# Split weight tiles laid out by parity, and the two matmuls of every second wide tile exchanged

## The chip, the cores and the metric

The kernel runs on one core of a Trainium2 chip. The time is that of the device in microseconds (us), the median of three executions; one further execution was taken with the hardware profiler. TensorE (PE in the profile) multiplies and has a second row, PEld, for its weight loads; VectorE (DVE) and ScalarE (ACT) work elementwise; SyncE (SP) issues the transfers. 

## The reference, cut to what matters

Two layers, each of a half-step SwiGLU feed-forward block, a mixer and a second feed-forward block, then a last norm. x has 256 positions of 1024 channels, float32.

```python
def swiglu_ffn(h, w_up, w_down):
    u = h @ w_up                      # 1024 -> 2 * 2816
    a, b = jnp.split(u, 2, axis=-1)
    return (jax.nn.silu(a) * b) @ w_down

for l in range(DEPTH):                # DEPTH = 2
    x = x + 0.5 * swiglu_ffn(rmsnorm(x, norm_ffn1[l]), ffn1_w_up[l], ffn1_w_down[l])
    x = x + hybrid_mixer(rmsnorm(x, norm_mix[l]), ...)   # in-projection, pooling, RG-LRU, gates, out-projection
    x = x + 0.5 * swiglu_ffn(rmsnorm(x, norm_ffn2[l]), ffn2_w_up[l], ffn2_w_down[l])
return rmsnorm(x, final_norm)
```

All matrices together are 3152 tiles of 128x128 float32 values, and each is used once.

## The kernel before, in words

Activations lie transposed: channels on the 128 partitions, the 256 positions along the free dimension. Every matrix tile is the stationary operand of TensorE (the weights), and the activations stream past it as the moving operand. Products are made in fp32r from two halves: each weight tile w is split into a high half wh (ScalarE, a copy that rounds to fp32r) and a low half wl = w - wh (VectorE), and each activation x into xh and xl in the same way. Three products count: wh*xh, wh*xl and wl*xh.

There are two forms of a tile's work. The wide form (`mm_wide`, feed-forward blocks and the mixer's last projection) uses that xh and xl of a block lie side by side: one matmul wl with the 256 columns of xh (L330), and one matmul wh with all 512 columns of xh and xl (L331), both into one PSUM bank; the sums of the bank's two halves are added later. The narrow form (`mm`, nearly all of the mixer) has three matmuls of 256 columns: wh*xh, wh*xl, wl*xh (L317, L318, L319). Each of these matmuls is preceded by a weight load of its own (LDWEIGHTS), which PE takes up while the matmul before it is still streaming.

The weights come in the order of their use, 8 tiles to a chunk (`CHUNK`), one DMA per chunk into one of 5 raw buffers (`NRAW`); a chunk is then split by one ScalarE and one VectorE instruction into one of 8 pairs of buffers wh and wl (`NSPL`). A matmul waits for its chunk's split, and a split waits until PE has gone through the chunk that had the buffer before.

The order of all instructions is made ahead by a planner (`Plan.schedule`) that simulates the engines with given durations: PE and the DMA queue keep the order of the program, ScalarE and VectorE take the ready operation with the longest work behind it.

Places in SBUF: the pool of the wh buffers comes first (each 4096 bytes a partition, a tile 512 bytes), then a filler of `SHIFT` = 112 floats (448 bytes), then the wl buffers, then XS, the activations of the block in work, and the other moving operands, each a multiple of 256 bytes long. Counted modulo 256 bytes, wl tiles lie where the moving operands lie, and wh tiles 64 bytes past it: from wh to wl there are 8 x 4096 + 448 bytes, which is 192 modulo 256, and from wl to XS 8 x 4096, which is 0.

The lines that the text names are L317 to L319 in `mm`, L330 and L331 in `mm_wide`, L220 (ScalarE) and L229 (VectorE) in the helpers, and L361, the norm's sum over channels, a float32 matmul that is put between two wide tiles.

Of the kernel before, what the change touches and what calls it, by code (L numbers as in the profile page):

```python
# [9 lines left out]
F32R = mybir.dt.float32r  # L10
# [25 lines left out]
CHUNK = 8  # L36
HEAD = [[2, 2, 4], [4, 4], [4, 4], [4, 4]]
NRAW = 5
NSPL = 8
SHIFT = 112  # L40
WARM = 7


# [155 lines left out]
class Trunk:  # L199
# [62 lines left out]
    def chunk(self, q):  # L262

        prev = self.raws[q - NRAW] if q >= NRAW else None
        raw = Buf(self.plan, lambda: self.env.rawp.tile([128, CHUNK * 128], F32, tag="raw", name="raw"), prev)
        prev_h, prev_l = self.spl[q - NSPL] if q >= NSPL else (None, None)
        hi = Buf(self.plan, lambda: self.env.whp.tile([128, CHUNK * 128], F32R, tag="wh", name="wh"), prev_h)
        lo = Buf(self.plan, lambda: self.env.wlp.tile([128, CHUNK * 128], F32R, tag="wl", name="wl"), prev_l)
        self.raws.append(raw)
        self.spl.append((hi, lo))  # L270
        return raw, hi, lo

    def chunk_run(self, q, o, n, d):
        raw = self.raws[q]
        hi, lo = self.spl[q]

        def load():
            self.env.nc.sync.dma_start(  # L278
                out=raw.t[:, o * 128:(o + n) * 128],
                in_=self.env.wts[d * 16384:(d + n) * 16384].rearrange("(p f) -> p f", p=128))  # L280

        s = slice(o * 128, (o + n) * 128)
        self.dma_in(load, 0.182 * n, [(raw, o)])
        self.split(lambda: hi.t[:, s], lambda: lo.t[:, s], lambda: raw.t[:, s], [(raw, o)], [(hi, o)], [(lo, o)], n * 128)
        for i in range(o, o + n):
            self.where.append((q, o, i))

# [12 lines left out]
    def next_tile(self, tag):  # L300
        c = len(self.order)
        self.order.append(tag)
        while c >= len(self.where):
            self.more_weights()
        q, o, i = self.where[c]
        hi, lo = self.spl[q]
        s = slice(i * 128, (i + 1) * 128)
        return lambda: hi.t[:, s], lambda: lo.t[:, s], [(hi, o), (lo, o)]

    def mm(self, tag, ps, half, xh, xl, r, start, stop):  # L310

        wh, wl, keys = self.next_tile(tag)

        def fn():
            t = self.env.nc.tensor
            out = ps.t[:, half, :]
            t.matmul(out, lhsT=wh(), rhs=xh(), start=start, stop=False)  # L317
            t.matmul(out, lhsT=wh(), rhs=xl(), start=False, stop=False)  # L318
            t.matmul(out, lhsT=wl(), rhs=xh(), start=False, stop=stop)  # L319

        self.plan.add("PE", T_MM, fn, keys + list(r), [(ps, half)])

    def mm_wide(self, tag, ps, x, r, start, stop):

        wh, wl, keys = self.next_tile(tag)

        def fn():
            t = self.env.nc.tensor

            t.matmul(ps.t[:, 0, :], lhsT=wl(), rhs=x()[:, 0, :], start=start, stop=False, skip_group_check=True)  # L330
            t.matmul(ps.t, lhsT=wh(), rhs=x(), start=False, stop=stop, skip_group_check=True)  # L331

        self.plan.add("PE", T_MM_WIDE, fn, keys + list(r), [(ps, 0), (ps, 1)])

# [44 lines left out]
    def x(self, m):  # L379
        return self.X.t[:, KD + m * S:KD + (m + 1) * S]  # L380
# [457 lines left out]
@with_exitstack  # L838
def tile_trunk(ctx: ExitStack, tc: tile.TileContext, xt: bass.AP, par: bass.AP, wts: bass.AP, out: bass.AP):
    trunk = Trunk()  # L840
    env = Env()
    env.nc, env.xt, env.par, env.wts, env.out = tc.nc, xt, par, wts, out
    env.one = ctx.enter_context(tc.tile_pool(name="one", bufs=1))
    env.rawp = ctx.enter_context(tc.tile_pool(name="rawp", bufs=NRAW))
    env.whp = ctx.enter_context(tc.tile_pool(name="whp", bufs=NSPL))


    ctx.enter_context(tc.tile_pool(name="shift", bufs=1)).tile([128, SHIFT], F32, name="shift")
    env.wlp = ctx.enter_context(tc.tile_pool(name="wlp", bufs=NSPL))
    env.xsp = ctx.enter_context(tc.tile_pool(name="xsp", bufs=1))  # L850
    env.big = ctx.enter_context(tc.tile_pool(name="big", bufs=1))
    env.psp = ctx.enter_context(tc.tile_pool(name="psp", bufs=8, space=bass.MemoryType.PSUM))
    trunk.env = env
    with tc.manual_schedule():
        for op in trunk.plan.schedule():
            op.fn()
# [52 lines left out]
```

## Time and profile before

| what | us |
|---|---|
| median of three executions | 1120.95 |
| the three | 1120.82, 1120.95, 1125.40 |
| the profiled execution | 1125.55 |
| its span, first to last instruction | 1123.8 |
| PE busy | 1111.3 |
| VectorE busy | 885.0 |
| ScalarE busy | 691.1 |

Wide tiles: 2218. Narrow tiles: 934. In a timeline, the start of a matmul tells more than its length: matmuls are pipelined, so the recorded lengths overlap, and the time that a matmul takes on PE is from its start to the start of the next one. A window count of a line includes the instruction that was already running when the window began.

### The profile page before, as it was taken

Reading aid. Unit: us, or ns where it says so; the run is one execution under the profiler, and the core shown is the slowest. Engines: PE = TensorE matmul, PEld = TensorE weight load, DVE = VectorE, ACT = ScalarE, POOL = GpSimd, SP = SyncE. Lnnn points to the kernel's source line nnn. Section 1 sums busy time; section 2 is a strip of 40 time slices with the busy share of each in tenths; the row PEclk is TensorE's granted clock in tenths of the full one; section 3 lists DMA queues with packets and bytes.
Section 4 is the critical chain, followed back from the end, with each engine's and each line's share of the span. In section 5 each row is a group of like instructions: output and inputs, shape, how many; then the busy total and the mean of one; then the engine's idle time right before and its main releaser. Section 6 shows DMA issues by size and latency. Waiting matters only on the chain.

```text
span 1123.8 us, 18938 instructions
## 1 busy us (share of the span) xinstructions
PE 1111.3 (99%) x7268; PEld 1017.0 (91%) x7268; DVE 885.0 (79%) x1384; ACT 691.1 (62%) x1133; POOL 0.2 (0%) x4
## 2 busy tenths in 40 slices
PE   8999999999999999999999999999999999999996
PEld 7888888999999888888888888899999998888886
DVE  7998766898987877776678887679989788777652
ACT  8766655568865755555566566555687666555541
POOL 0000000000000000000000000000000000000000
PEclk9999999999999999999999999999999999999999
DMA  8856666556556666666666666666475565656531
GB/s 286 264 171 206 189 188 188 184 174 200 188 183 192 182 192 188 187 188 188 187 188 195 197 190 192 198 188 190 141 227 183 183 197 184 189 187 189 188 107 38
DMA packets 59130, 210.03 MB, mean 187 GB/s; under 512 B 6560, under 2 KB 7456, under 8 KB 59040
## 3 DMA queue, kind: packets, MB, share of 16 engines
q1 hardware_dynamic: 59040, 208.82, 59.7%
q8 instruction: 57, 0.93, 0.3%
q14 instruction: 33, 0.27, 0.1%
HBM read 207.75 MB, written 1.05 MB: 186 GB/s over the span
## 4 chain that ended last, share of the span: by engine, by line
PE 98%; DVE 0%; DMA 0%; ACT 0%; SPq 0%; DVEq 0%; issue 0%; ACTq 0%
PE ps L331 45%; PE ps L330 23%; PE ps L318 10%; PE ps L317 10%; PE ps L319 10%; DMA XG<-in_x 0%; PE ps L361 0%; DVE XF L229 0%; DVE rt L371 0%; ACT XS L220 0%; SPq L278 0%; SPq L792 0%; PE ps L367 0%; DVE wl L229 0%; ACT wh L220 0%; DVEq L904 0%
## 5 line engine op out<-in xcount | busy, mean ns | idle before, releaser
L220 ACT ACTIVATE wh<-raw 128x1024 fp32r<-128x1024 f32 (+2 forms) x399 | 418.0, 1050 | 364.1 <-PE ps L331 271.3
L229 DVE TENSOR_TENSOR wl<-raw,wh 128x1024 fp32r<-128x1024 f32 (+2 forms) x399 | 481.8, 1210 | 184.9 <-ACT wh L220 183.4
L331 PE MATMUL ps<-XS,wh 128*128 128x512 f32 x1408 | 491.7, 394 | 0.0
L330 PE MATMUL ps<-XS,wl 128*128 128x256 f32 x1408 | 396.2, 281 | 2.5 <-DVE wl L229 2.5
L331 PEld LDWEIGHTS ps<-XS,wh 128*128 128x128 f32 x1408 | 265.5, 189 | 58.4
L330 PEld LDWEIGHTS ps<-XS,wl 128*128 128x128 f32 x1408 | 267.6, 190 | 3.7 <-DVE wl L229 3.6
L317 PE MATMUL ps<-XS,wh 128*128 128x256 f32 x640 | 180.2, 282 | 0.0
L318 PE MATMUL ps<-XS,wh 128*128 128x256 f32 x640 | 179.9, 281 | 0.0
L319 PE MATMUL ps<-XS,wl 128*128 128x256 f32 x640 | 179.9, 281 | 0.0
L317 PEld LDWEIGHTS ps<-XS,wh 128*128 128x128 f32 x640 | 122.8, 192 | 0.1
L318 PEld LDWEIGHTS ps<-XS,wh 128*128 128x128 f32 x640 | 120.2, 188 | 0.1
L319 PEld LDWEIGHTS ps<-XS,wl 128*128 128x128 f32 x640 | 120.1, 188 | 0.0
L331 PE MATMUL ps<-GA,wh 128*128 128x512 f32 x341 | 119.9, 393 | 0.0
L331 PE MATMUL ps<-GB,wh 128*128 128x512 f32 x341 | 119.9, 393 | 0.0
L330 PE MATMUL ps<-GB,wl 128*128 128x256 f32 x341 | 95.4, 280 | 0.0
L330 PE MATMUL ps<-GA,wl 128*128 128x256 f32 x341 | 95.4, 280 | 0.0
L331 PEld LDWEIGHTS ps<-GA,wh 128*128 128x128 f32 x341 | 64.0, 188 | 14.1
L331 PEld LDWEIGHTS ps<-GB,wh 128*128 128x128 f32 x341 | 64.1, 188 | 14.0
L229 DVE TENSOR_TENSOR FT<-ps,FT 128x256 f32<-128x256 f32 x176 | 72.8, 416 | 2.4 <-ACT FT L220 2.4
L220 ACT ACTIVATE FT<-ps 128x256 f32<-128x256 f32 x176 | 64.1, 366 | 6.1 <-PE ps L331 5.8
L330 PEld LDWEIGHTS ps<-GB,wl 128*128 128x128 f32 x341 | 64.6, 189 | 0.0
L330 PEld LDWEIGHTS ps<-GA,wl 128*128 128x128 f32 x341 | 64.5, 189 | 0.0
(127 smaller groups left out, 1228.7 us busy)
## 6 DMA issues: line engine op xcount, KB each, us to landing
raw<-in_w SPq DMA_DIRECT2D x390, 512.0 KB, 4.1
raw<-in_w SPq DMA_DIRECT2D x7, 256.0 KB, 5.4
XG<-in_x SPq DMA_DIRECT2D x3, 256.0 KB, 5.1
out<-XF SPq DMA_DIRECT2D x3, 256.0 KB, 2.2
raw<-in_w SPq DMA_DIRECT2D x2, 128.0 KB, 3.1
out<-XF SPq DMA_DIRECT2D x2, 128.0 KB, 2.1
XG<-in_x SPq DMA_DIRECT2D x1, 132.0 KB, 2.6
XG<-in_x SPq DMA_DIRECT2D x1, 128.0 KB, 3.4
```

Of the source, the lines that this page charges most:

```text
L220: self.env.nc.scalar.activation(out=out(), in_=in_(), func=func, scale=scale if isinstance(scale, float) else scale(), **kw)
L229: return self.dve(t_dve(n), lambda v: v.tensor_tensor(out=out(), in0=a(), in1=b(), op=op), r, w)
L317: t.matmul(out, lhsT=wh(), rhs=xh(), start=start, stop=False)
L318: t.matmul(out, lhsT=wh(), rhs=xl(), start=False, stop=False)
L319: t.matmul(out, lhsT=wl(), rhs=xh(), start=False, stop=stop)
L330: t.matmul(ps.t[:, 0, :], lhsT=wl(), rhs=x()[:, 0, :], start=start, stop=False, skip_group_check=True)
L331: t.matmul(ps.t, lhsT=wh(), rhs=x(), start=False, stop=stop, skip_group_check=True)
```

## The change

Three things change. First, high and low buffers come from one pool of 7 pairs, each buffer 144 x 8 floats (4608 bytes), and the filler before XS has 48 floats (192 bytes). Second, within a buffer the 8 tiles of a chunk are laid out by parity: even tiles (0, 2, 4, 6) one after another from the start, odd tiles one after another from 560 floats (2240 bytes) on. Modulo 256 bytes the moving operands now lie 192 past the start of a buffer (14 x 4608 + 192), an even tile, high or low, is 64 bytes past the moving operands' place, and an odd tile is at it (2240 is 192 modulo 256). The split instructions write in the order (pair, parity, 128 floats). Third, in the wide form even tiles run the low matmul (256 columns) and then the high one (512), odd tiles the high one and then the low one.

```diff
--- before.py
+++ after.py
@@ -36,8 +36,9 @@
 CHUNK = 8
 HEAD = [[2, 2, 4], [4, 4], [4, 4], [4, 4]]
 NRAW = 5
-NSPL = 8
-SHIFT = 112
+NSPL = 7
+SHIFT = 48
+ODD = 560
 WARM = 7
 
 
@@ -264,8 +265,8 @@
         prev = self.raws[q - NRAW] if q >= NRAW else None
         raw = Buf(self.plan, lambda: self.env.rawp.tile([128, CHUNK * 128], F32, tag="raw", name="raw"), prev)
         prev_h, prev_l = self.spl[q - NSPL] if q >= NSPL else (None, None)
-        hi = Buf(self.plan, lambda: self.env.whp.tile([128, CHUNK * 128], F32R, tag="wh", name="wh"), prev_h)
-        lo = Buf(self.plan, lambda: self.env.wlp.tile([128, CHUNK * 128], F32R, tag="wl", name="wl"), prev_l)
+        hi = Buf(self.plan, lambda: self.env.splp.tile([128, CHUNK * 144], F32R, tag="wh", name="wh"), prev_h)
+        lo = Buf(self.plan, lambda: self.env.splp.tile([128, CHUNK * 144], F32R, tag="wl", name="wl"), prev_l)
         self.raws.append(raw)
         self.spl.append((hi, lo))
         return raw, hi, lo
@@ -281,7 +282,14 @@
 
         s = slice(o * 128, (o + n) * 128)
         self.dma_in(load, 0.182 * n, [(raw, o)])
-        self.split(lambda: hi.t[:, s], lambda: lo.t[:, s], lambda: raw.t[:, s], [(raw, o)], [(hi, o)], [(lo, o)], n * 128)
+
+        def by_parity(t):
+
+            return t[:, 0:2 * ODD].rearrange("p (a c) -> p a c", a=2)[:, :, o * 64:(o + n) * 64].rearrange(
+                "p a (i c) -> p i a c", c=128)
+
+        self.split(lambda: by_parity(hi.t), lambda: by_parity(lo.t),
+                   lambda: raw.t[:, s].rearrange("p (i a c) -> p i a c", a=2, c=128), [(raw, o)], [(hi, o)], [(lo, o)], n * 128)
         for i in range(o, o + n):
             self.where.append((q, o, i))
 
@@ -304,12 +312,13 @@
             self.more_weights()
         q, o, i = self.where[c]
         hi, lo = self.spl[q]
-        s = slice(i * 128, (i + 1) * 128)
-        return lambda: hi.t[:, s], lambda: lo.t[:, s], [(hi, o), (lo, o)]
+        at = ODD * (i % 2) + 128 * (i // 2)
+        s = slice(at, at + 128)
+        return lambda: hi.t[:, s], lambda: lo.t[:, s], [(hi, o), (lo, o)], i % 2
 
     def mm(self, tag, ps, half, xh, xl, r, start, stop):
 
-        wh, wl, keys = self.next_tile(tag)
+        wh, wl, keys, odd = self.next_tile(tag)
 
         def fn():
             t = self.env.nc.tensor
@@ -322,13 +331,19 @@
 
     def mm_wide(self, tag, ps, x, r, start, stop):
 
-        wh, wl, keys = self.next_tile(tag)
+        wh, wl, keys, odd = self.next_tile(tag)
 
         def fn():
             t = self.env.nc.tensor
 
-            t.matmul(ps.t[:, 0, :], lhsT=wl(), rhs=x()[:, 0, :], start=start, stop=False, skip_group_check=True)
-            t.matmul(ps.t, lhsT=wh(), rhs=x(), start=False, stop=stop, skip_group_check=True)
+
+            for low in ((False, True) if odd else (True, False)):
+                first = start and low != odd
+                last = stop and low == odd
+                if low:
+                    t.matmul(ps.t[:, 0, :], lhsT=wl(), rhs=x()[:, 0, :], start=first, stop=last, skip_group_check=True)
+                else:
+                    t.matmul(ps.t, lhsT=wh(), rhs=x(), start=first, stop=last, skip_group_check=True)
 
         self.plan.add("PE", T_MM_WIDE, fn, keys + list(r), [(ps, 0), (ps, 1)])
 
@@ -842,11 +857,10 @@
     env.nc, env.xt, env.par, env.wts, env.out = tc.nc, xt, par, wts, out
     env.one = ctx.enter_context(tc.tile_pool(name="one", bufs=1))
     env.rawp = ctx.enter_context(tc.tile_pool(name="rawp", bufs=NRAW))
-    env.whp = ctx.enter_context(tc.tile_pool(name="whp", bufs=NSPL))
+    env.splp = ctx.enter_context(tc.tile_pool(name="splp", bufs=NSPL))
 
 
     ctx.enter_context(tc.tile_pool(name="shift", bufs=1)).tile([128, SHIFT], F32, name="shift")
-    env.wlp = ctx.enter_context(tc.tile_pool(name="wlp", bufs=NSPL))
     env.xsp = ctx.enter_context(tc.tile_pool(name="xsp", bufs=1))
     env.big = ctx.enter_context(tc.tile_pool(name="big", bufs=1))
     env.psp = ctx.enter_context(tc.tile_pool(name="psp", bufs=8, space=bass.MemoryType.PSUM))
```

PE, in one group of the first feed-forward block's up-projection: where one PSUM tile (ps_413) ends and the next (ps_419) begins, before the change.

```order
L330 MATMUL ps_413<-XS_83,wl_331 128x256
L331 MATMUL ps_413<-XS_83,wh_330 128x512
L330 MATMUL ps_419<-XS_83,wl_358 128x256
L331 MATMUL ps_419<-XS_83,wh_357 128x512
L330 MATMUL ps_419<-XS_83,wl_358 128x256
```

The same block after the change, one PSUM tile (ps_565) of 8 weight tiles from its first matmul to the first of the next; x2 is two in a row.

```order
L344 MATMUL ps_565<-XS_80,wl_555 128x256
L346 MATMUL ps_565<-XS_80,wh_554 128x512 x2
L344 MATMUL ps_565<-XS_80,wl_555 128x256 x2
L346 MATMUL ps_565<-XS_80,wh_554 128x512 x2
L344 MATMUL ps_565<-XS_80,wl_555 128x256 x2
L346 MATMUL ps_565<-XS_80,wh_554 128x512 x2
L344 MATMUL ps_565<-XS_80,wl_555 128x256 x2
L346 MATMUL ps_565<-XS_80,wh_554 128x512 x2
L344 MATMUL ps_565<-XS_80,wl_555 128x256
L344 MATMUL ps_591<-XS_80,wl_584 128x256
```

The number of matmuls is the same; 256 and 512 columns no longer alternate but come in pairs, and the pair of low matmuls runs across the end of a PSUM tile too.

ScalarE at the start of the first mixer, before the change: the norm's square root (sd), the table, and the splits of weight chunks (wh<-raw) between the mixer's own work.

```order
L220 ACTIVATE wh<-raw 128x1024
L220 ACTIVATE sd<-ps,eps 128x256
L220 ACT_TABLE_LOAD
L220 ACTIVATE dummy<-eps 128x1
L220 ACTIVATE wh<-raw 128x1024 x6
L220 ACTIVATE PHL<-MB 128x256 x2
L220 ACTIVATE wh<-raw 128x1024
L220 ACTIVATE PHL<-MB 128x256 x2
L220 ACTIVATE V<-U,prm 128x256 x2
```

The same place after the change.

```order
L221 ACTIVATE wh<-raw 128x4x2x128
L221 ACTIVATE sd<-ps,eps 128x256
L221 ACT_TABLE_LOAD
L221 ACTIVATE dummy<-eps 128x1
L221 ACTIVATE wh<-raw 128x4x2x128 x6
L221 ACTIVATE PHL<-MB 128x256 x2
L221 ACTIVATE wh<-raw 128x4x2x128
L221 ACTIVATE PHL<-MB 128x256 x2
L221 ACTIVATE V<-U,prm 128x256 x2
```

The instructions stand as they stood; a split has the same 1024 values, written as 4 x 2 runs of 128.

## Rows read from the trace of the kernel before

**Rows 1.** The profile page: busy time of each engine, its share of the span and its instructions.
```profile
PE 1111.3 (99%) x7268; PEld 1017.0 (91%) x7268; DVE 885.0 (79%) x1384; ACT 691.1 (62%) x1133; POOL 0.2 (0%) x4
```

**Rows 2.** The page's chain of the work that ended last, its share of the span by engine and then by line.
```profile
PE 98%; DVE 0%; DMA 0%; ACT 0%; SPq 0%; DVEq 0%; issue 0%; ACTq 0%
PE ps L331 45%; PE ps L330 23%; PE ps L318 10%; PE ps L317 10%; PE ps L319 10%; DMA XG<-in_x 0%; PE ps L361 0%; DVE XF L229 0%; DVE rt L371 0%; ACT XS L220 0%; SPq L278 0%; SPq L792 0%; PE ps L367 0%; DVE wl L229 0%; ACT wh L220 0%; DVEq L904 0%
```

**Rows 3.** Groups of instructions by line and form: all wide tiles (one L331 each). After the count: busy us, mean ns of one, idle us before them.
```profile
L331 PE MATMUL ps<-XS,wh 128*128 128x512 f32 x1408 | 491.7, 394 | 0.0
...
L331 PE MATMUL ps<-GA,wh 128*128 128x512 f32 x341 | 119.9, 393 | 0.0
L331 PE MATMUL ps<-GB,wh 128*128 128x512 f32 x341 | 119.9, 393 | 0.0
...
L331 PE MATMUL ps<-MU,wh 128*128 128x512 f32 x64 | 23.0, 395 | 0.0
L331 PE MATMUL ps<-MI,wh 128*128 128x512 f32 x64 | 23.0, 394 | 0.0
```

**Rows 4.** Timeline of PE and its loads in the first feed-forward block: start us, length us, engine, line, operation.
```profile
40.33 0.28 PE L330 MATMUL ps<-XS,wl 128*128 128x256 f32 x1
40.33 0.19 PEld L331 LDWEIGHTS ps<-XS,wh 128*128 128x128 f32 x1
...
40.45 0.39 PE L331 MATMUL ps<-XS,wh 128*128 128x512 f32 x1
40.45 0.19 PEld L330 LDWEIGHTS ps<-XS,wl 128*128 128x128 f32 x1
...
40.68 0.28 PE L330 MATMUL ps<-XS,wl 128*128 128x256 f32 x1
...
40.79 0.40 PE L331 MATMUL ps<-XS,wh 128*128 128x512 f32 x1
```

**Rows 5.** The same view in the second layer's first feed-forward block.
```profile
600.13 0.28 PE L330 MATMUL ps<-XS,wl 128*128 128x256 f32 x1
600.14 0.19 PEld L331 LDWEIGHTS ps<-XS,wh 128*128 128x128 f32 x1
...
600.25 0.39 PE L331 MATMUL ps<-XS,wh 128*128 128x512 f32 x1
600.25 0.19 PEld L330 LDWEIGHTS ps<-XS,wl 128*128 128x128 f32 x1
...
600.47 0.28 PE L330 MATMUL ps<-XS,wl 128*128 128x256 f32 x1
```

**Rows 6.** Stretches of 140 us inside the four feed-forward blocks, L331 alone (one to a wide tile): busy us and count on PE and PEld, granted clock, DMA share, GB/s.
```profile
25.00:165.00 140.00, 140.00 (x401) 75.15 (x401) 1.00 0.65 204
400.00:540.00 140.00, 140.00 (x401) 75.16 (x400) 1.00 0.62 188
580.00:720.00 140.00, 140.00 (x413) 77.34 (x412) 1.00 0.63 195
940.00:1080.00 140.00, 140.00 (x402) 75.15 (x401) 1.00 0.62 190
```

**Rows 7.** The same view of the whole stretch between the norm at 568 us and the second mixer.
```profile
569.00:749.00 180.00, 175.46 (x516) 96.71 (x516) 1.00 0.63 193
```

**Rows 8.** Timeline of PE around that norm's sum (L361).
```profile
568.06 0.28 PE L330 MATMUL ps<-XS,wl 128*128 128x256 f32 x1
568.18 0.39 PE L331 MATMUL ps<-XS,wh 128*128 128x512 f32 x1
568.41 0.59 PE L361 MATMUL ps<-acc,ones 128*128 128x256 f32 x2
568.65 0.47 PE L330 MATMUL ps<-XS,wl 128*128 128x256 f32 x1
```

**Rows 9.** Stretches of 140 us inside the two mixers, L317 alone (one to a narrow tile); columns as in rows 6.
```profile
200.00:340.00 140.00, 111.32 (x397) 76.12 (x397) 1.00 0.59 186
755.00:895.00 140.00, 111.37 (x397) 76.08 (x397) 1.00 0.60 188
```

**Rows 10.** Timeline of PE soon after the start, in the first block.
```profile
14.99 0.28 PE L330 MATMUL ps<-XS,wl 128*128 128x256 f32 x1
...
15.34 0.28 PE L330 MATMUL ps<-XS,wl 128*128 128x256 f32 x1
...
15.70 0.28 PE L330 MATMUL ps<-XS,wl 128*128 128x256 f32 x1
```

**Rows 11.** The raw weight buffers: what ended the idle time of the engine before the splits (us, times), and who waited for the splits.
```profile
  PE ps L331: 271.3, 245
...
  PE ps L330: 2.5, 3
```

**Rows 12.** Groups by form: the splits of a whole chunk, and two VectorE operations on 512 values, of which the first reads a broadcast operand in two runs.
```profile
L229 DVE TENSOR_TENSOR wl<-raw,wh 128x1024 fp32r<-128x1024 f32 x390 | 476.2, 1223 | 184.3 <-ACT wh L220 183.0
L220 ACT ACTIVATE wh<-raw 128x1024 fp32r<-128x1024 f32 x390 | 412.9, 1061 | 363.9 <-PE ps L331 271.3 <-PE ps L318 57.0 <-issue 26.7
...
L229 DVE TENSOR_TENSOR MB<-ps,rt 128x512 f32<-128x512 f32 x20 | 13.3, 682 | 1.4 <-PE ps L319 1.4
...
L229 DVE TENSOR_TENSOR TT<-TT,V 128x512 f32<-128x512 f32 x10 | 6.8, 681 | 0.0
```

**Rows 13.** Busy time of every engine over the second mixer: PE, PEld, DVE, ACT, POOL with counts, granted clock, DMA share, GB/s.
```profile
748.00:904.00 156.00, 156.00 (x1325) 155.95 (x1325) 139.16 (x208) 106.43 (x152) 0.00 (x0) 1.00 0.60 186
```

## The prediction

> **What bounds the kernel now.** I read the page first: PE is busy for 1111.3 of 1123.8 us [rows 1], and the chain that ended last is 98% PE, all of it matmuls of L330, L331 and L317 to L319 [rows 2]. So only what changes the step from one matmul to the next on PE can move the time. Then I took the timelines of PE, reading starts and not lengths. In the first block a wide tile is 0.12 us from the low matmul to the high one and 0.23 us to the next tile, 0.35 us together [rows 4]; every load starts with the matmul before it and lasts 0.19 us by its record. In the second layer's first block the same two lines on the same operands make 0.12 and 0.22, 0.34 together [rows 5]. [...] Narrow tiles take 140 us / 396 = 353.5 ns in both mixers [rows 9].
>
> This is the reading on which the forecast rests. The 10 ns are not work: 768 columns pass in either case, and code, tiles and places in SBUF are the same. The rate changes at one point: after 568.18 us two passes of the norm's sum stand between two wide tiles [rows 8], and from there to the mixer, 516 tiles [rows 7], the faster rate holds. The other norms leave the slower rate as it was. So a stretch of wide tiles settles in one of at least two rhythms, and which one depends on the moment at which loads and streams meet. What the slower rhythm costs is most easily explained as loads and moving operands getting in each other's way in SBUF. That is an inference; no row shows a bank.
>
> The four times of the same program fit: 1125.55 (profiled) and 1125.40 on one side, 1120.95 and 1120.82 on the other. The 4.6 us between are 460 tiles at 10 ns, about one block's worth of wide tiles. So the profiled execution had one block in the fast rhythm, and the median probably two.
>
> **The change part by part.** Of the 3152 tiles 2218 are wide, 1408 + 2 x 341 + 2 x 64 [rows 3], and 934 narrow.
>
> The order. Per pair of tiles there were two steps of 256 columns and two of 512, and there are the same four afterwards; 256, 512, 512, 256 instead of 256, 512, 256, 512. Priced by the rows of before, 2 x 118 + 2 x 232 = 700 ns (0.12 and 0.23 in [rows 4], exact to the 350 of [rows 6]), it costs and saves nothing.
>
> The places. Before, a load under the 256 columns is of wh, 64 bytes past the moving operand's place, and a load under the 512 columns is of wl, at it. After, the loads under 256 columns are of even tiles (64 past) and those under 512 of odd tiles (at it). So each kind of step keeps the kind of load that it had; the order changes which kinds follow each other. A sum over steps is again nothing, and any gain or loss has to come from the rhythm. Its bounds from the rows: if all tiles now at 350 run at 340, (2218 - 516) x 10 ns = 17.0 us are gained; if every wide tile runs like a narrow one, 1702 x 3.5 + 516 x 13.5 = 12.9 us are lost. That such a slow rhythm exists for wide tiles too is seen soon after the start, 14.99 to 15.70 for two tiles, 355 ns each [rows 10].
>
> I take the 340. The reason: in the slow rhythm every tile has a short step whose load has to be ready within 118 ns, so the meeting of load and stream is set anew at each tile. In pairs, two steps of 512 columns follow each other, and under each the load (0.19 us by its record [rows 4]) fits into the step with time to spare; for about 460 ns nothing re-times the stream, and it can find the clear spacing that the block at 580 us shows. I hold this for somewhat likelier than not to help, no more, since the pair of short steps is the opposite case.
>
> [...]
>
> Narrow tiles. Their order stays, but the places change: of three loads one was at the moving operand's place and two were 64 past; now an even tile's first two following loads are 64 past and its third is at, an odd tile's the other way round. Both mixers run at one rate [rows 9], even the second, right behind the fast wide stretch, so I see no sign that place alone frees them. Value 0; bounds 934 x 13.5 = 12.6 us gained (if they reach 340), and the same lost if a load at the wrong place costs as much as the whole present excess.
>
> One buffer pair fewer. A chunk feeds 8 x 0.35 = 2.8 us of PE, so 7 pairs hold 19.6 us of work. ScalarE's idle time before splits is 271.3 us of waiting for PE to give a buffer back, and PE waited 2.5 us for splits in all [rows 11]: the ring is full, and the splits are not short of time. Even the second mixer leaves VectorE 139.16 busy of 156 us [rows 13]. Value 0; the upper bound is those waits doubled, 2.5 us.
>
> The split's runs of 128. VectorE takes 682 ns for 512 values in two runs and 681 in one [rows 12], so a break between runs costs about 1 ns; 8 runs add perhaps 8 ns to 1223 (ScalarE: 1061), hidden while the ring is full. Without that cover it would matter at once, since 1223 of 2800 ns are taken.
>
> The sum: 1125.55 (the profiled execution; span 1123.8 and 1.75 around it) - 17.0 = 1108.5, and that is 12.4 us under the median of 1120.95.
>
> **The rivals.** First, nothing changes: the rhythms come as before, by chance at each norm. For it: the sum over steps is zero, and the wide code has two rhythms at equal places, so place and order may both be beside the point. Against it: pairs are another sequence and need not have the same rhythms. One block fast gives 1125.6, two 1120.9, three 1116: 1116 to 1126, and 1131 with none. [...] The trace neither shows a conflict nor explains without one why the same code has two rates.
>
> Second, slower: the pairs of 256-column steps behave like narrow code. There 256-column steps follow each other without end and never found a faster rhythm than 353.5 [rows 9]; now two follow each other at each second tile boundary, with a load that has to fit under each, and the fast rhythm of the one block is lost as well. Price 12.9 us: 1125.55 + 12.9 = 1138.4. It decides against the change as soon as the mean wide tile exceeds today's (1702 x 350 + 516 x 340) / 2218 = 347.7 ns. Against it: the two long steps between.
>
> Third, the narrow tiles gain too, because half of them now have all their loads at one place: another 12.6 us, 1096.
>
> **How the numbers follow.** Forecast (wide tiles at 340 in most or all stretches) 0.41, by itself 1104 to 1115; with the narrow ones too 0.06; as before 0.27; slower like narrow code 0.26, of which half lies above 1138. A measurement of this kernel can tell about 0.5%, 5.6 us, from no change: faster is below 1115.3, slower above 1126.6. Faster: 0.41 + 0.06, less 0.02 for a forecast that comes only in part, plus 0.01 of the second case: 0.46. Same: most of the second case and that part, 0.23. Slower: 0.26 + 0.05 of the second case with no block fast: 0.31. The range runs from 1099 to 1138: it leaves out the third rival and the upper half of the slower one, 0.19.
>
> **What would show it.** Windows of 140 us in the blocks: 412 wide tiles in each means the forecast, 400 in some the first rival, 396 or fewer the second. Timelines of PE: the two short steps in a row at 113 ns each or at 118; the two long ones at 227 or at 232. L317's count in 140 us above 396 would be the third rival. The ring: PE's waits for VectorE's splits must stay near 2.5 us; if they grow in the mixers, my zero for the eighth buffer is wrong. VectorE's mean for a split far above 1223 ns would make the 8 ns wrong. The forecast is wrong as a whole if pairs settle in a rhythm that the trace of before doesn't have.

## The result, and the profile after

| | us |
|---|---|
| before, median (5 executions) | 1121.07 |
| after, median (5 executions, 1132.2 to 1134.6) | 1133.48 |
| ratio | 1.0096, 95% interval 1.0073 to 1.0119 |
| profiled execution before, after | 1125.55, 1132.20 |

The change makes the kernel about 1% slower. The five executions of the kernel before fall in two groups, near 1121 and near 1125.5; the five of the changed kernel do not. The page after has the same shape as before: PE is the bound, the other engines have the work that they had ([rows 1, 2] answer to these lines).

Page of the changed kernel, busy time and chain:

```profile
PE 1117.1 (99%) x7268; PEld 1015.2 (90%) x7268; DVE 885.4 (78%) x1384; ACT 690.3 (61%) x1133; POOL 0.2 (0%) x4
...
PE 98%; DMA 0%; DVE 0%; ACT 0%; SPq 0%; DVEq 0%; issue 0%; ACTq 0%
```

The wide tiles, counted in the same stretches as in [rows 6] (L346 is now the matmul of 512 columns, one to a tile; busy and count on PE and PEld, clock, DMA share, GB/s):

```profile
25.00:165.00 140.00, 125.58 (x401) 60.74 (x401) 1.00 0.65 203
400.00:540.00 140.00, 125.65 (x401) 60.74 (x400) 1.00 0.61 188
580.00:720.00 140.00, 125.68 (x401) 60.74 (x400) 1.00 0.62 188
940.00:1080.00 140.00, 125.68 (x402) 60.73 (x400) 1.00 0.62 187
```

Take off the one that was already running: 400 in each, 350 ns a tile, in all four blocks. The block that held 412 before now holds 400. The granted clock is 1.00 in all four, as it was at 350 and at 340 before [rows 6], so the 10 ns are not the clock. Inside a pair of tiles the timeline of PE shows how the 700 ns are spread (x2 are two in a row; the answer to [rows 5]):

```profile
600.19 0.40 PE L344 MATMUL ps<-XS,wl 128*128 128x256 f32 x2
600.42 0.63 PE L346 MATMUL ps<-XS,wh 128*128 128x512 f32 x2
600.89 0.40 PE L344 MATMUL ps<-XS,wl 128*128 128x256 f32 x2
601.12 0.63 PE L346 MATMUL ps<-XS,wh 128*128 128x512 f32 x2
```

0.23 us for two short steps, 0.47 for two long ones, 0.70 together: the two steps of 256 and the two of 512 cost in pairs what they cost alternating. Only ahead of the first norm's sum (L376) is it otherwise in this profile:

```profile
17.96 0.39 PE L344 MATMUL ps<-XS,wl 128*128 128x256 f32 x2
...
18.64 0.39 PE L344 MATMUL ps<-XS,wl 128*128 128x256 f32 x2
...
19.44 0.59 PE L376 MATMUL ps<-acc,ones 128*128 128x256 f32 x2
...
19.98 0.63 PE L346 MATMUL ps<-XS,wh 128*128 128x512 f32 x2
...
20.68 0.63 PE L346 MATMUL ps<-XS,wh 128*128 128x512 f32 x2
```

A pair takes 0.68 us before that sum, 340 ns a tile, and 0.70 behind it. So pairs can run at the fast rate, and here the norm ends it. The narrow tiles (L326, the answer to [rows 9]) are slower:

```profile
200.00:340.00 140.00, 110.73 (x393) 75.30 (x393) 1.00 0.60 185
760.00:900.00 140.00, 110.66 (x394) 75.39 (x393) 1.00 0.59 186
```

393 to 394 less one instead of 396: their starts repeat every 1070 ns for three tiles, 356.7 a tile, where they had 353.3. So the difference of the two profiled executions has two parts: 516 tiles that lost 10 ns, 5.2 us, and 934 that lost 3.3 ns, 3.1 us; the first narrow tile of the changed kernel starts 1.5 us earlier, at 193.47 instead of 195.03 us, and takes that much off: 6.8, measured 6.65. The earlier start is already there at the first norm's sum (19.44 instead of 21.00 us). In both profiles PE had waited for a split until shortly before 10 us (1.78 us until 9.46, 2.10 us until 9.78); then the granted clock was 0.50 in the one before and 1.00 in the one after (PE, busy and count, clock, DMA share, GB/s; before, then after):

```profile
9.50:12.50 3.00, 3.00 (x10) 0.50 1.06 410
9.50:12.50 3.00, 2.72 (x15) 1.00 1.05 404
```

The medians lie further apart than the profiles: the profiled execution before is 4.5 us above its median, by about what one more fast block gives (shown below on another kernel), and the profiled one after is 1.3 us below its own. With both, 6.65 becomes the 12.4 us of the table.

### The profile page after: what moved, and what is told of

The parts are those of the page before. It is cut to its first block, busy times and chain, and to the rows that moved or that the text cites. A ratio compares the mean times of both kernels' runs of the same rounds, so it can differ in the third digit from the quotient of the medians.

```text
span 1130.4 us, 18877 instructions
## 1 busy us (share of the span) xinstructions
PE 1117.1 (99%) x7268; PEld 1015.2 (90%) x7268; DVE 885.4 (78%) x1384; ACT 690.3 (61%) x1133; POOL 0.2 (0%) x4
## 4 chain that ended last, share of the span: by engine, by line
PE 98%; DMA 0%; DVE 0%; ACT 0%; SPq 0%; DVEq 0%; issue 0%; ACTq 0%
PE ps L346 46%; PE ps L344 23%; PE ps L327 10%; PE ps L328 10%; PE ps L326 10%; DMA XG<-in_x 0%; PE ps L376 0%; DVE XF L230 0%; DVE rt L386 0%; ACT XS L221 0%; SPq L279 0%; SPq L807 0%; PE ps L382 0%; DVE wl L230 0%; DVEq L918 0%
## 5 line engine op out<-in xcount | busy, mean ns | idle before, releaser
L346 PE MATMUL ps<-XS,wh 128*128 128x512 f32 x1408 | 442.1, 395 | 0.0
L344 PE MATMUL ps<-XS,wl 128*128 128x256 f32 x1408 | 281.5, 280 | 3.4 <-DVE wl L230 3.4
L346 PEld LDWEIGHTS ps<-XS,wh 128*128 128x128 f32 x1408 | 213.8, 188 | 0.1
L326 PE MATMUL ps<-XS,wh 128*128 128x256 f32 x640 | 180.8, 283 | 0.0
L328 PE MATMUL ps<-XS,wl 128*128 128x256 f32 x640 | 180.5, 282 | 0.0
L326 PEld LDWEIGHTS ps<-XS,wh 128*128 128x128 f32 x640 | 122.9, 192 | 0.1
L327 PEld LDWEIGHTS ps<-XS,wh 128*128 128x128 f32 x640 | 121.5, 190 | 0.1
L346 PE MATMUL ps<-GB,wh 128*128 128x512 f32 x341 | 109.6, 395 | 0.0
L346 PE MATMUL ps<-GA,wh 128*128 128x512 f32 x341 | 109.5, 395 | 0.0
L344 PE MATMUL ps<-GB,wl 128*128 128x256 f32 x341 | 70.1, 279 | 0.0
L344 PE MATMUL ps<-GA,wl 128*128 128x256 f32 x341 | 70.1, 279 | 0.0
L230 DVE TENSOR_TENSOR FT<-FT,rt 128x512 f32<-128x512 f32 x88 | 60.3, 685 | 0.1
L346 PEld LDWEIGHTS ps<-GA,wh 128*128 128x128 f32 x341 | 52.9, 188 | 0.0
```

What stands on the lines that cost most here:

```text
L230: return self.dve(t_dve(n), lambda v: v.tensor_tensor(out=out(), in0=a(), in1=b(), op=op), r, w)
L344: t.matmul(ps.t[:, 0, :], lhsT=wl(), rhs=x()[:, 0, :], start=first, stop=last, skip_group_check=True)
L346: t.matmul(ps.t, lhsT=wh(), rhs=x(), start=first, stop=last, skip_group_check=True)
```

## The experiments

Theory A is that place and order decide which rhythms the steps of PE can settle in, and that a break (a float32 matmul between two tiles: the norm's sum, or a short one put in) decides which one they settle in. Its rivals are named with the runs. In all kernels with short matmuls of ones, these are added work whose result the tile's own first matmul overwrites.

**Places alone, order alone.** The first run undoes the order (each wide tile low, then high); the second leaves the places and the 8 buffers of before and takes the order alone.

```diff
# e1_layout_only, against the changed kernel, in mm_wide
-            for low in ((False, True) if odd else (True, False)):
...
+            t.matmul(ps.t[:, 0, :], lhsT=wl(), rhs=x()[:, 0, :], start=start, stop=False, skip_group_check=True)
+            t.matmul(ps.t, lhsT=wh(), rhs=x(), start=False, stop=stop, skip_group_check=True)
```

> The new places and the 7 buffer pairs, with the old order of the wide tiles (low, high, in every tile). Theory A (the order in pairs takes away the fast rhythm of 340 ns, the places by parity slow the narrow tiles from 353.5 to 356.7 ns): narrow tiles 356.7 ns, 393 in 140 us; some block of wide tiles can be at 340 again; 1122 to 1134. Rival B (places alone do both): every wide tile at 350 or slower, as in the changed kernel, and 1131 or more. Rival C (7 buffers or writing in runs of 128): PE's waits for splits grow beyond 3 us, narrow tiles with gaps between chunks.

> The old places and 8 buffer pairs, with the order in pairs. Theory A: narrow tiles back at 353.5 ns (396 in 140 us), no block of wide tiles at 340, all at 350; 1131 = 1125.55 + 516 x 10 ns. Rival B (places alone): a block at 340 can be there and the time is as before, 1121 to 1126. Rival C: also as before.

Measured: places alone 1125.99, ratio 1.0034 (1.0015 to 1.0053); order alone 1144.98, ratio 1.0198 (1.0166 to 1.0230). Wide tiles (L340) and narrow ones (L326) with the places alone:

```profile
400.00:540.00 140.00, 112.77 (x405) 75.80 (x405) 1.00 0.63 189
...
200.00:340.00 140.00, 110.70 (x394) 75.44 (x393) 1.00 0.59 186
```

And wide (L336) and narrow (L318, one to a tile) with the order alone:

```profile
400.00:540.00 140.00, 124.42 (x394) 60.57 (x394) 1.00 0.60 185
...
200.00:340.00 140.00, 111.05 (x395) 74.19 (x396) 1.00 0.60 185
```

The narrow part is settled: 356.7 ns come with the new places and go with them, whatever the order (by their starts 356.7 with the places alone, 353.3 with the order alone). For the wide tiles no theory had the right numbers: places alone bring 346.7 ns in every block (404 in 140 us), a rate that neither kernel shows; the order alone brings 356.6 (393). The order is bad with the old places, where half of the loads then fall under another kind of step than they did; in the changed kernel the new places undo that, back to 350. The times fit: with the order alone every wide tile has 356.6 instead of the mixture of 350 and 340.

**Is the rhythm a matter of the break?** Both kernels get short float32 matmuls of 21 to 125 columns at many tile boundaries.

```diff
+    def breath(self, ps, g):
+        n = 16 + 13 * g % 112
+        self.plan.add(
+            "PE", 0.4,
+            lambda: self.env.nc.tensor.matmul(ps.t[:, 0, 0:n], lhsT=self.ones.t, rhs=self.ones.t[:, 0:n], start=True, stop=True),
+            [(self.ones, 0)], [(ps, 0)])
...
+                    if j % 2 == 0 and h == 0:
+                        self.breath(ps[j, h], j // 2)
...
+            self.breath(pm, 10 + m)
```

> The kernel before with 18 short float32 matmuls of ones in each feed-forward block (at the start of every second j and of every output tile m; 16 to 120 columns wide, overwritten by the tile's own first matmul), so that the rhythm is drawn anew about 70 times. If the rhythm is chance (theory A): after some of them 340, after others 350 or 353.5, a quarter or so at 340. If the fast rate belongs to a place in the program (rival D: something else runs in the second layer's first block): 340 there alone, whatever stands in between. 1121 + 72 x 0.4 = 1150, less 10 ns for each tile that is faster.

> The changed kernel with the same short matmuls. Theory A in its strong form (pairs have no fast rhythm): no stretch at 340 after any of some 70 draws. In its weak form (pairs have it, but find it more seldom): some at 340, fewer than in the kernel before with the same draws. 1133 + 29 = 1162.

Measured, one execution each: 1135.65 and 1129.19. The changed kernel became faster than it was, with 72 short matmuls more. In the kernel before with these draws, 36 of the 72 stretches behind a short matmul ran at 340 ns a tile and 36 at 350, and each stretch kept one rate to its end. The same short matmul at the same place led to the same rate in all four blocks: with 81 columns or more always 340, with 73 or fewer 350 except 55 columns, which gave 340. That one, behind 42 columns and 350 ns:

```profile
42.07 0.28 PE L330 MATMUL ps<-XS,wl 128*128 128x256 f32 x1
...
42.42 0.32 PE L340 MATMUL ps<-ones 128*128 128x55 f32 x2
...
42.99 0.28 PE L330 MATMUL ps<-XS,wl 128*128 128x256 f32 x1
...
43.33 0.28 PE L330 MATMUL ps<-XS,wl 128*128 128x256 f32 x1
```

So within this execution it isn't chance, and it isn't a place in the program (rival D falls). In the changed kernel every stretch behind a short matmul of any length ran at 340 (341 behind 29 columns); wide tiles with no short matmul between them and the last norm stayed at 350. One short matmul and its surroundings there:

```profile
41.92 0.28 PE L344 MATMUL ps<-XS,wl 128*128 128x256 f32 x1
42.04 0.32 PE L355 MATMUL ps<-ones 128*128 128x55 f32 x2
42.17 0.37 PE L344 MATMUL ps<-XS,wl 128*128 128x256 f32 x1
42.38 0.62 PE L346 MATMUL ps<-XS,wh 128*128 128x512 f32 x2
42.84 0.39 PE L344 MATMUL ps<-XS,wl 128*128 128x256 f32 x2
43.06 0.62 PE L346 MATMUL ps<-XS,wh 128*128 128x512 f32 x2
```

From 42.38 to 43.06 a pair of tiles takes 0.68 us. The short matmul costs 0.13 us up to the next start and another 0.09 in that next step (0.21 instead of 0.12), some 0.2 together, where the expectations had 0.4; the times come out lower for that too. The pairs do have the fast rhythm: the strong form of theory A falls, and the weak form (more seldom) with it.

**One break to a stretch.** Six short matmuls of 120 columns, one behind each norm of the feed-forward blocks (at j = 2) and one before each last projection of the mixer.

```diff
+                    if j == 2 and h == 0:
+                        self.breath(ps[j, h], 120)
...
+        self.breath(ps[0], 120)
```

> The kernel before with six short float32 matmuls of ones, 120 columns each: at the first tile of j = 2 in each feed-forward block and at the first tile of each last projection of the mixer. In the run with many short matmuls those of 81 columns and more were all followed by tiles of 340 ns. Theory A (a break sets the rhythm, and the rhythm holds until the next break): 340 ns from each of the six on, also through the down projections; 412 wide tiles in 140 us in all four blocks. About 2218 - 4 x 32 - 24 = 2060 tiles at 340 instead of 516: 1125.55 - 15.4 + 6 x 0.4 = 1112.5. Rival E (a short matmul is needed again and again): the tiles fall back to 350 after some groups, 1120 or more.

> The changed kernel with the same six short matmuls. Theory A: pairs have the rhythm of 340 ns and lack only the right start, so the same 2060 tiles run at 340: 1133.5 - 20.6 + 2.4 = 1115.3, faster than the kernel before; narrow tiles stay at 356.7. Rival F (the pairs got 340 only because short matmuls came so often): back at 350, 1133 or more.

Measured: the kernel before with the six 1111.64, ratio 0.9907 (0.9877 to 0.9937); the changed kernel with the six 1113.42, ratio 0.9911 (0.9885 to 0.9937). Wide tiles of the changed kernel with the six:

```profile
25.00:165.00 140.00, 126.72 (x413) 61.90 (x412) 1.00 0.67 207
400.00:540.00 140.00, 126.83 (x412) 61.86 (x412) 1.00 0.64 194
580.00:720.00 140.00, 126.82 (x413) 61.93 (x412) 1.00 0.63 193
932.00:1072.00 140.00, 126.81 (x413) 61.97 (x412) 1.00 0.64 194
```

Both came within 2 us of what theory A said. In the profiles the rhythm holds for 500 tiles until the next float32 break; rivals E and F fall. With the right start the two kernels' wide tiles are equal. But the start isn't sure in each execution: two of the five of the kernel before with the six took 1115.5 and 1115.7 us, against 1110.2 to 1111.6 of the others. By estimate, 4 to 5 us at 10 ns a tile, that is one block of wide tiles at 350; no profile shows such an execution.

**Narrow tiles.** The same kind of short matmul in the mixer, in both kernels (`self.breath(ps, 16 + 6 * (c // 2) % 112)` at the start of `win_pair`).

> The kernel before with a short float32 matmul of 18 to 124 columns at the start of each pair of narrow output tiles in the mixer (18 in each mixer). Theory A (every sequence has several rhythms): some of the pairs at 340 ns a tile instead of 353.5. If narrow code has one rhythm only: 353.5 everywhere, and 1121 + 36 x 0.4 = 1135.

> The changed kernel with the same short matmuls in the mixer. Theory A: some pairs of output tiles off 356.7 ns, towards 340. If the odd tiles' place fixes the excess (rival B for the narrow tiles): 356.7 in all of them and 1133.5 + 14 = 1148.

Measured, one execution each: 1134.96 and 1141.72. Behind every one of the short matmuls the narrow tiles were back at 353.3 in the one kernel and at 356.7 in the other. The longest stretch between two of them has 67 tiles from the first of these lines to the second, and from the third to the fourth in the changed kernel:

```profile
256.93 0.28 PE L319 MATMUL ps<-XS,wl 128*128 128x256 f32 x1
...
280.61 0.28 PE L319 MATMUL ps<-PHL,wl 128*128 128x256 f32 x1
...
256.19 0.28 PE L328 MATMUL ps<-XS,wl 128*128 128x256 f32 x1
...
280.08 0.28 PE L328 MATMUL ps<-PHL,wl 128*128 128x256 f32 x1
```

With these places none of the 18 lengths changes anything: the places set the rate of narrow tiles. So the next runs change places alone: all tiles 64 bytes past the moving operands' place, all at it, and, in the old order with the six short matmuls, all 64 and all 128 past.

```diff
# h1_all_past; h2_all_at has SHIFT = 64 besides
-ODD = 560
+ODD = 512
# h3_old_order_all_past, against the kernel before with the six; h4: SHIFT2 = 32
-SHIFT = 112
+SHIFT = 64
+SHIFT2 = 48
...
+    ctx.enter_context(tc.tile_pool(name="shift2", bufs=1)).tile([128, SHIFT2], F32, name="shift2")
```

SHIFT2 is a second filler, between the low buffers and XS.

> The changed kernel with the odd tiles also 64 bytes past the moving operands' place (ODD 512 instead of 560): order in pairs, 7 buffers and runs of 128 stay. If the odd tiles' place costs the narrow tiles their 3.3 ns: narrow tiles at 353.5 or less, 396 or more in 140 us. If mixing places is what costs: also less than 356.7. If 7 buffers or the runs do it: 356.7 stays. The wide tiles: the load under 512 columns is then 64 past; 350 if its place doesn't matter, more (the order alone had 356.7) if it does.

> The changed kernel with every tile at the moving operands' place (ODD 512, SHIFT 64). If a load at that place under 256 columns is what costs: narrow tiles slower than 356.7, about 360 (three loads of three instead of half); if the mixture costs: 353.5 or less. Wide tiles: the low and high loads under 256 columns lose their 64 bytes, 350 or more.

> The old order with 8 buffers and the six short matmuls, high and low tiles both 64 bytes past the moving operands' place. Narrow tiles as in the run with all tiles 64 past. Wide tiles: 340 again after the short matmuls if the rhythm doesn't hang on the place of the load under 512 columns; if it does, 346 to 357. With 340 and 353.5 it is the 1111.6 of the run with the six alone; with narrow tiles at 340 it would be 1099.

> The same with all tiles 128 bytes past. If places count by how far a load lies ahead of the stream, 128 past is another case than 64 and at: narrow tiles anything from 340 to 360, and the wide tiles' 340 may be gone. If only at costs and everything else is free: as 64 past.

Measured: 1121.02, 1131.59, 1137.52, 1136.82, one execution each. The changed kernel with its odd tiles moved on to 64 past as well, and nothing else, takes as long as the kernel before. Narrow tiles (L326) with all at the place:

```profile
200.00:340.00 140.00, 110.05 (x390) 74.69 (x389) 1.00 0.59 184
```

389 in 140 us, 360 ns, as expected of "at costs". With all 64 past, in the middle of the mixer, and in a timeline of the first narrow tiles, ahead of the norm:

```profile
200.00:340.00 140.00, 111.36 (x397) 76.09 (x397) 1.00 0.60 186
```

```profile
192.27 0.28 PE L326 MATMUL ps<-XS,wh 128*128 128x256 f32 x1
...
192.61 0.28 PE L326 MATMUL ps<-XS,wh 128*128 128x256 f32 x1
...
192.95 0.28 PE L326 MATMUL ps<-XS,wh 128*128 128x256 f32 x1
...
193.29 0.28 PE L326 MATMUL ps<-XS,wh 128*128 128x256 f32 x1
```

353.3 once more in the middle; but 0.34 us a tile for the 12 narrow tiles between the wide ones and the norm, and so for the 22 of the last output tile, a rate that narrow code had nowhere before. All 128 past: 356.0. For wide tiles in the old order 340 was gone with all 64 past (353.3, 396 in 140 us, L332) and with all 128 past (351), although the six short matmuls were there:

```profile
400.00:540.00 140.00, 140.00 (x397) 74.49 (x397) 1.00 0.62 186
```

With all 64 past, only the load under 512 columns has another place than before. So the fast rhythm hangs on that place too, at least behind these six; other lengths weren't tried there. Wide tiles in pairs had 346.7 ns with all 64 past, and 348.3 with all at the place (L346), where 350 or more was expected:

```profile
400.00:540.00 140.00, 126.22 (x403) 61.20 (x402) 1.00 0.62 189
```

That is less than the 350 of the changed kernel, in which only half of the loads lie there. For wide tiles it is no sum of costs by load; narrow ones had 353.3, 356.7 and 360 ns with a third, half and all of their loads at the place, but 353.3 with none as well.

**Can a break lead narrow tiles to 340?** These two runs join the places of h1 and h3 with the short matmuls of e7 and with the six.

> The changed kernel with all tiles 64 bytes past, the six short matmuls before wide tiles and one of 18 to 124 columns before each pair of narrow output tiles in the mixer. Theory A (narrow code has a rhythm of 340 too, where all its loads are 64 past; a float32 break draws it anew): some of the pairs of output tiles at 340, the others at 353.5; wide tiles at 346.7 or 340. Rival G (340 in narrow code is only what is left over from the wide tiles before it, and no float32 break leads to it): 353.5 after every short matmul. 1121 + 17 = 1138 less 13 ns for each narrow tile at 340, less up to 7 ns for each wide one.

> The same draws with the old order and all tiles 64 bytes past (8 buffers, six short matmuls before wide tiles). The narrow tiles' instructions and places are those of the run before this one, so theory A expects the same share of pairs at 340 as there; wide tiles at 353.3 as without the draws: 1137.5 + 14 = 1151.5 less 13 ns for each narrow tile at 340.

Measured, one execution each: 1122.67 and 1138.10. Behind 32 of the 36 short matmuls of the mixers in the first run, and 30 of 36 in the second, narrow tiles ran at 340 until the next break; the others led to 353.3, and so did the norm's own break. Two stretches without a break in them, in the old order (L318):

```profile
257.00:279.00 22.00, 17.89 (x65) 12.11 (x65) 1.00 0.65 206
326.00:354.00 28.00, 22.75 (x83) 15.44 (x83) 1.00 0.61 194
```

82 tiles in 28 us are 341 ns. Rival G falls. The wide tiles in pairs stayed at 346.7 with all 64 past, behind the six as well.

**Both rhythms in one kernel, and the ring.** The low tiles of chunks of narrow tiles are moved 64 bytes on, the others stay; 7 buffers; the six short matmuls and one of 88 columns in each mixer. The second run has 7 buffers and nothing else.

```diff
# b1_best, against the kernel before with the six
-NSPL = 8
+NSPL = 7
...
+        lo = Buf(self.plan, lambda: self.env.wlp.tile([128, CHUNK * 128 + 64], F32R, tag="wl", name="wl"), prev_l)
...
+        self.past.append(16 if self.narrow else 0)
...
-        return lambda: hi.t[:, s], lambda: lo.t[:, s], [(hi, o), (lo, o)]
+        lo_at = slice(i * 128 + self.past[q], (i + 1) * 128 + self.past[q])
+        return lambda: hi.t[:, s], lambda: lo.t[:, lo_at], [(hi, o), (lo, o)]
...
+            if c == C_LRU:
+                self.breath(ps, 88)
```

> The old order with 7 buffers; high tiles 64 past, low tiles at the moving operands' place in chunks of wide tiles and 64 past in chunks of narrow tiles; the six short matmuls of 120 columns before wide tiles and one of 88 before the second pair of output tiles of each mixer. Theory A (place and break together choose the rhythm, chunk by chunk): wide tiles at 340 behind the short matmuls as with the six alone, narrow tiles at 340 from the short matmul on: 1111.6 - (934 - 2 x 34 - 22) x 13.3 ns + 2 x 0.4 = 1101.2. If the mixed places break the narrow rhythm: 1112.

> The kernel before with 7 pairs of buffers instead of 8 and nothing else. Theory A: the eighth buffer is worth nothing, 1121 to 1126 as before, PE's waits for splits at 2.5 to 3.5 us. Rival C (the ring is part of the 12 us): PE's waits grow, 1127 or more.

Measured: b1 1099.87, ratio 0.9816 (0.9789 to 0.9844), 1.3 us from what was expected, and faster than both kernels (one of its six executions took 1106.20 us, the others 1099.2 to 1101.1); 7 buffers alone 1120.67, ratio 0.9997 (0.9977 to 1.0018), so rival C has no share. Narrow tiles of b1 (L321), and its wide ones (L336):

```profile
204.00:344.00 140.00, 113.69 (x412) 77.26 (x413) 1.00 0.62 193
745.00:885.00 140.00, 113.62 (x412) 77.15 (x411) 1.00 0.62 195
...
400.00:540.00 140.00, 140.00 (x413) 77.34 (x412) 1.00 0.63 194
```

The profile of the run with 7 buffers happened to be an execution of 1120.60. Its ten times fall in the two groups of the kernel before, and it shows what they are (L331, as in [rows 6]):

```profile
25.00:165.00 140.00, 140.00 (x413) 77.27 (x412) 1.00 0.66 208
400.00:540.00 140.00, 140.00 (x401) 75.14 (x401) 1.00 0.61 188
570.00:710.00 140.00, 140.00 (x413) 77.33 (x412) 1.00 0.63 195
930.00:1070.00 140.00, 140.00 (x401) 75.14 (x400) 1.00 0.61 188
```

Two blocks at 340 here, one in the 1125.55 of [rows 6]; the 496 tiles of the first block behind its norm, at 10 ns, are the 4.95 us between the two.

## Why the prediction was wrong

**The reading of the rhythms was right.** "A stretch of wide tiles settles in one of at least two rhythms" and "a block's worth of wide tiles" between the two groups of times: the draws and the profile with two fast blocks show both. That breaks set it was right too. "By chance at each norm" holds only in part: in the run with the draws the same short matmul led to the same rate in all four blocks, but the first norm's break led to 350 in the profile of before and to 340 in that with 7 buffers.

**The step that failed** is "I take the 340", with its reason that under two long steps in a row "nothing re-times the stream, and it can find the clear spacing". The pairs don't drift into the fast rhythm: in the changed kernel all 2186 wide tiles behind the first norm stay at 350. They have the fast rhythm and keep it for hundreds of tiles, but something must start it, and the norm's break, which starts it in one or two blocks of the kernel before, does not: behind pairs at 340 it led back to 350, at 19.44 us of the profile after and at each later norm of the changed kernel with the six. I mistook the existence of a fast rhythm for a tendency towards it. The sum over steps, "costs and saves nothing", was the better forecast for the 1702 tiles that were slow; for the 516 fast ones the loss stood in the first rival ("1131 with none").

**The narrow tiles** had the value 0 and bounds of 12.6 us to both sides; it was 3.1 us of loss. The reason for 0, "no sign that place alone frees them", asked only whether place could help. The runs: 353.3 with one load of three at the moving operands' place, 356.7 with half of them, 360 with all. With none 353.3 again, but a break can then bring 340. 1131 plus 3.1 is 1134.1; measured 1133.48.

**The slower rival** (wide pairs like narrow code, 1138) did not come in the changed kernel (with the order alone, at the old places, pairs had 356.6); the third rival (narrow tiles gain) neither.

**The ring and the runs of 128** had the value 0: 7 buffers alone cost nothing, and PE's waits for the splits went from 2.5 [rows 11] to 2.9 us with them and to 3.4 in the changed kernel. VectorE's split took 1224 ns on the mean instead of 1223, so the breaks between runs cost 1 ns and not 8.

**Place alone.** PE's instructions for narrow tiles and their order were the same in the changed kernel and in the two that only move its tiles, and the rate was 353.3 ns with all loads 64 past, 356.7 with half of them at the place and 360 with all of them (and, with all 64 past, 340 behind a break): PE does lose time by where its two operands lie. No stretch of any run went below 340 ns a tile, with two matmuls or with three.

What stays open: what inside the chip makes the rhythms (that it is the moment at which loads and streams meet, and that they get in each other's way in SBUF, was my inference, and no run shows it), why the norm's break starts the fast one in some blocks only and never in pairs, and which part of the short matmul (its length, its load, its own place) decides. What stands ahead of a break may count: ahead of the first norm the tiles ran at 353 ns in the profile of before (350 behind it) and at 350 in that with 7 buffers (340 behind it). Other distances than 0, 64 and 128 bytes weren't tried, and no run separates places modulo 256 bytes from places modulo another number.

## What to carry to other kernels

When PE is the bound, count tiles in equal stretches before explaining anything: two rates of the same code in one trace (here 350 and 340 ns) can mean a state that can be set (here by a short float32 matmul). A rate that occurs somewhere is no forecast that a change will reach it; ask what started it there, and try the start by itself (here eight short matmuls of some 0.2 us, with places chosen for each form of tile, were worth 1.8%, and the reordering gained nothing in any run). And when one layout serves two forms of work, price the move for both.

## What the runs showed of the hardware

- In these kernels the step of a fp32r matmul hangs on where the tile being loaded lies against the tile being streamed. Narrow tiles, three matmuls of 256 columns each: 360 ns with all loads at the same place modulo 256 bytes, 356.7 with half, 353.3 with a third or none (the others 64 bytes past), 356.0 with all 128 bytes past, 340 with all 64 past and the right start.
- Wide tiles, 256 and 512 columns: 340, 346.7, 348.3, 350, 351, 353.3 and 356.6 ns were seen, each constant over hundreds of tiles as places, order and breaks had it, all at a granted clock of 1.00.
- In the kernel before, a float32 matmul of 55 columns between two tiles moved all following tiles from 350 to 340 ns until the next such break; behind one of 42 or 68 columns tiles ran at 350.
- The best rate was 340 ns for 768 columns, for two matmuls and for three alike.
